# Two state recurrences written ahead of the score products in a step of gated linear attention

## The chip, the cores and the metric

The kernel runs on one core of a Trainium2 chip. The metric is the device time of one execution in microseconds (us); a kernel's time is the median of several executions. The engines of a core run side by side, each in the order of its own list of instructions, and wait for one another by semaphores: TensorE (PE; its weight loads are shown as PEld), VectorE (DVE), ScalarE (ACT), GpSimd (POOL) and SyncE (SP), which issues most of the DMAs.

## What is computed

Two layers of a streaming encoder over 1024 new frames and 64 frames of a running stream. In each layer half of the heads are gated linear attention (GLA), half are differential attention; a projection, a normalised residual and a convolutional feed-forward part follow. The change lies in GLA, which the reference computes in blocks of 64 tokens (cut):

```python
def gla_chunked(q, k, v, log_a, s0):
    G = jnp.cumsum(log_a, axis=-2)
    q_dec = q * jnp.exp(G)
    k_inv = k * jnp.exp(-G)
    k_end = k * jnp.exp(G_last - G)
    A = jnp.where(causal, jnp.einsum('nbhid,nbhjd->nbhij', q_dec, k_inv), 0.0)
    o_intra = jnp.einsum('nbhij,nbhjv->nbhiv', A, v)
    upd = jnp.einsum('nbhjd,nbhjv->nbhdv', k_end, v)
    decay = jnp.exp(G_last[..., 0, :])
    def step(S, inp):
        dec, u, qd = inp
        o = jnp.einsum('bhid,bhdv->bhiv', qd, S)
        return dec[..., None] * S + u, o
    s_final, o_inter = lax.scan(step, s0, (decay, upd, q_dec))
    o = o_intra + o_inter
```

The output is then normalised per head and multiplied by a gate. Everything is float32; the large projections are split into a high and a low part and computed in three passes of products.

## The kernel before

The kernel is one long program, with the order of every engine's work written out by hand. Python generators write it: a main loop writes blocks of large products, and between blocks a pump takes the next step of a generator that runs beside them, paced by an estimate of TensorE's and VectorE's time. The program's order on an engine is the order in which instructions are written. The waits between engines are put in from the order of writing: an instruction waits for what was written ahead of it in the program and touches the same memory. For PSUM a bank counts as a whole here, as the waits in the lists show.

`gla(l, p)` is such a generator. It runs four times, for layers 0 and 1 and for the pairs of heads p = 0 and 1, beside a projection's blocks of 24 products of 256 columns (`vd_block`, and at its end other projections). It has 15 steps, i = 0 to 14; a step writes some of ten stages, each for the tile of 128 tokens that lies `lag` steps back (nine tiles; the last is the running stream's). One step stands after each block of large products. The stages that matter here, with tile t:

- s0 (lag 0, TensorE): a transpose of the decayed keys, and two score products q·k of 128 columns, one for each head, into columns 0 to 127 of banks `bk(t, 0)` and `bk(t, 1)`. In the trace each float32 product is two passes, so s0's two products are four.
- s1 (lag 1, TensorE): the four products k·v that update the state, into columns 128 to 255 of the same two banks.
- v1 (lag 2, VectorE): two recurrences S = decay·S + update, the second from the result of the first, each reading columns 128 to 255 of one of the banks and writing a slot of the state (SR, a part of ACC).
- s2 (lag 2, TensorE): four products q·S from those states and two products of the masked scores with v, into columns 256 to 383.
- v2, v2b, v2c, s3 and v3 (lags 3 to 6): gating, the norm's power on GpSimd, scaling, transposes of the output, and their split into high and low parts.
- v0 (lag 0, VectorE and ScalarE): the masked copy of the scores out of both banks, and a copy of the transposed keys.

Banks alternate with the tile, so that the tiles i and i - 2 share theirs:

```python
        def bk(t, i):
            return 4 + 2 * (t % 2) + i
```

Beside the stages, VectorE also takes the low part of a weight (WL = RAW - WH, 128x1024) off its list where the pump puts it, behind v0 of two steps in each call.

Of the kernel before, what the change touches and what calls it, by code (L numbers as in the profile page):

```python
# [45 lines left out]
def hybrid_kernel(ctx: ExitStack, tc: tile.TileContext,  # L46
# [672 lines left out]
    def gla(l, p):  # L719
# [92 lines left out]
            V.scalar_tensor_tensor(ML[:, 2 * p:2 * p + 2, t0:t0 + n], src, gn, f(hi), ALU.mult, ALU.subtract)  # L812


        stages = ((s0, 0), (s1, 1), (v1, 2), (v2c, 5), (s2, 2), (v2b, 4), (s3, 6), (v2, 3), (v3, 6), (v0, 0))
        for i in range(9 + 6):
            for fn, lag in stages:
                if 0 <= i - lag < 9:
# [505 lines left out]
    for l in range(DEPTH):  # L1324
# [89 lines left out]
        def vd_block(s, t):  # L1414
            tm_block(L["vd%d" % s], t, 256, ev_vd(l, s, t))

        beside(gla(l, 0))
        for t in range(9):
            vd_block(0, t)
# [27 lines left out]
        drain()  # L1447
        ring["banks"] = (0, 1, 2)
        beside(gla(l, 1))
        pump()  # L1450
        for t in range(9):
# [175 lines left out]
```

## Time and profile before

| | us |
|---|---|
| median of 3 executions | 2831.58 (2826.98 to 2833.05) |
| the profiled execution | 2822.54 |
| its span, first to last instruction | 2820.8 |
| TensorE matmul busy, weight loads busy | 2779.2 (99%), 2709.6 (96%) |
| VectorE busy | 1695.0 (60%) |
| ScalarE busy | 1150.7 (41%) |
| chain that ended last: TensorE, VectorE | 92%, 2% |

In the profile an engine's busy time counts only its own operations, and the ends of matmuls are modelled. Idle time stands with the operation that follows it, with the engine that released it. The chain of work that ended last follows the program back from its last instruction, at each step to what released it.

### The profile page before, as it was taken

To read this page: it belongs to the slowest core of one execution; us is meant where nothing else is said; L and a number is where in the kernel's file an instruction comes from. 1 tells how busy PE (TensorE), PEld (TensorE's weight loads), DVE (VectorE), ACT (ScalarE), POOL (GpSimd) and SP (SyncE) were. 2 spreads that over 40 slices of the span, in tenths; PEclk is the share of its full clock that TensorE was granted. 3 is DMA by queue.
4 is the path that set the end of the run, shared out by engine and by line. 5 is a ranking of instruction groups with operands and counts; after the bars stand their busy time and mean duration, and the time that the engine had idled before them with its cause. 6 is when DMAs were issued, how large, how long until landed. Compare 5 with 4: busy or idle time off the path is not lost.

```text
span 2820.8 us, 46613 instructions
## 1 busy us (share of the span) xinstructions
PE 2779.2 (99%) x18407; PEld 2709.6 (96%) x18407; DVE 1695.0 (60%) x4104; ACT 1150.7 (41%) x2432; POOL 234.7 (8%) x387
## 2 busy tenths in 40 slices
PE   8999999999999999999999999999999999999999
PEld 8999888999999999999999898889999999999999
DVE  5443458477566666666772333685766666666665
ACT  5333348555322222222454242684552222222235
POOL 2200024200000000000021000340000000000000
PEclk9999999999999999999999999999999999999999
DMA  7421176341111111111352213834321111111122
GB/s 245 141 69 47 54 188 151 119 131 56 48 42 45 45 45 46 45 45 46 113 197 82 61 35 90 214 85 146 105 64 46 45 46 46 45 46 45 45 90 84
DMA packets 250690, 235.47 MB, mean 83 GB/s; under 512 B 12974, under 2 KB 225416, under 8 KB 250472
## 3 DMA queue, kind: packets, MB, share of 16 engines
q1 hardware_dynamic: 233032, 189.62, 23.4%
q0 software_dynamic: 10656, 39.07, 3.9%
q10 hardware_dynamic: 6784, 3.81, 0.5%
q8 instruction: 145, 2.38, 0.3%
q14 instruction: 73, 0.60, 0.1%
HBM read 174.34 MB, written 58.11 MB: 82 GB/s over the span
## 4 chain that ended last, share of the span: by engine, by line
PE 92%; DVE 2%; issue 2%; DMA 2%; ACT 1%; POOL 0%; SPq 0%; ACTq 0%; DVEq 0%; POOLq 0%
PE PS L103 89%; PE PS L107 3%; DVE ACC L122 1%; DVE SML L122 1%; DMA WH<-KSd 0%; ACT ACC L1070 0%; DMA XS<-ACC 0%; DMA RAW<-in_w_in_dram 0%; DMA WH<-QSd 0%; DMA out_dram<-TMP 0%; DVE TMP L122 0%; DMA QSd<-MH 0%; DVE ML L122 0%; ACT WH L275 0%; DMA ACC<-in_x_prompt_dram 0%
## 5 line engine op out<-in xcount | busy, mean ns | idle before, releaser
L103 PE MATMUL PS<-XL,WH 128*128 128x384 f32 (+1 forms) x2976 | 557.3, 326 | 0.0
L103 PEld LDWEIGHTS PS<-XL,WH 128*128 128x128 f32 x2976 | 499.2, 188 | 0.0
L103 PE MATMUL PS<-XH,WH 128*128 128x384 f32 (+1 forms) x2592 | 484.7, 328 | 3.4 <-DVE TMP L122 3.4
L103 PE MATMUL PS<-XH,WL 128*128 128x384 f32 (+1 forms) x2592 | 478.9, 326 | 0.0
L103 PEld LDWEIGHTS PS<-XH,WH 128*128 128x128 f32 x2592 | 433.8, 188 | 4.7 <-DVE TMP L122 4.3
L103 PEld LDWEIGHTS PS<-XH,WL 128*128 128x128 f32 x2592 | 433.7, 188 | 0.1
L103 PE MATMUL PS<-MH,WH 128*128 128x384 f32 (+1 forms) x1248 | 387.2, 329 | 0.0
L103 PE MATMUL PS<-MH,WL 128*128 128x384 f32 (+1 forms) x1248 | 385.1, 327 | 0.0
L103 PE MATMUL PS<-ML,WH 128*128 128x384 f32 (+1 forms) x1248 | 384.3, 327 | 0.0
L122 DVE TENSOR_TENSOR TMP<-PS,RB 128x384 f32<-128x384 f32 (+2 forms) x376 | 159.6, 444 | 343.2 <-PE PS L103 329.1
L275 ACT ACTIVATE WH<-RAW 128x1024 fp32r<-128x1024 f32 (+2 forms) x209 | 216.7, 1048 | 336.0 <-PE PS L103 300.1
L1237 ACT ACTIVATE TMP<-TMP,VC 128x384 f32<-128x384 f32 (+1 forms) x264 | 183.1, 694 | 404.3 <-DVE TMP L122 403.5
L122 DVE TENSOR_TENSOR ACC<-PS,ACC 128x384 f32<-128x384 f32 (+1 forms) x456 | 239.7, 533 | 133.4 <-PE PS L103 132.7
L122 DVE TENSOR_TENSOR WL<-RAW,WH 128x1024 fp32r<-128x1024 f32 (+2 forms) x209 | 253.9, 1216 | 98.6 <-ACT WH L275 98.6
L122 DVE SCALAR_TENSOR_TENSOR TMP<-TMP,VC 128x384 f32<-128x384 f32 (+1 forms) x528 | 311.8, 591 | 0.1
L103 PEld LDWEIGHTS PS<-MH,WL 128*128 128x128 f32 x1248 | 230.9, 188 | 0.0
L103 PEld LDWEIGHTS PS<-ML,WH 128*128 128x128 f32 x1248 | 230.9, 188 | 0.0
L103 PEld LDWEIGHTS PS<-MH,WH 128*128 128x128 f32 x1248 | 230.1, 188 | 0.7 <-issue 0.3
L122 DVE TENSOR_REDUCE SML<-PS 128x1 f32<-128x384 f32 (+6 forms) x144 | 104.3, 724 | 41.9 <-PE PS L103 40.4
L103 PE MATMUL PS<-WH,XH 128*128 128x256 f32 (+1 forms) x864 | 128.4, 291 | 0.0
L1258 ACT ACTIVATE MH<-TMP 128x384 fp32r<-128x384 f32 x132 | 67.0, 508 | 135.6 <-DVE TMP L122 135.5
L103 PE MATMUL PS<-WH,XL 128*128 128x256 f32 (+1 forms) x864 | 122.0, 284 | 0.0
(202 smaller groups left out, 3440.9 us busy)
## 6 DMA issues: line engine op xcount, KB each, us to landing
RAW<-in_w_ffn_up_dram SPq DMA_DIRECT2D x88, 512.0 KB
RAW<-in_w_in_dram SPq DMA_DIRECT2D x48, 512.0 KB
RAW<-in_w_ffn_down_dram SPq DMA_DIRECT2D x44, 512.0 KB
RAW<-in_w_out_dram SPq DMA_DIRECT2D x32, 512.0 KB
XH<-XS SPq DMA_DIRECT2D x8, 1536.0 KB
XS<-ACC POOLq DMA_DIRECT2D x6, 1536.0 KB, 6.8
XH<-KSd SPq DMA_DIRECT2D x32, 256.0 KB
XH<-XS SPq DMA_DIRECT2D x4, 1280.0 KB
```

Of the source, the lines that this page charges most:

```text
L103: nc.tensor.matmul(out, lhsT, rhs, **kw)
L107: nc.tensor.transpose(out, in_, idn)
L122: return op(out, *a, **kw)
L275: act(hi, src, AF.Copy)
L1237: act(c, e[:, 0:w], AF.Identity, bias=cb(l, u), scale=cw(l, 0, u))
L1258: act(MH[:, mid["j"] % 4, mid["t0"]:mid["t0"] + n], y[:, :n], AF.Copy)
```

## The change

In the list of stages v1 is written first in a step, ahead of s0 and s1, and no longer behind them:

```diff
@@ -812,7 +812,7 @@
-        stages = ((s0, 0), (s1, 1), (v1, 2), (v2c, 5), (s2, 2), (v2b, 4), (s3, 6), (v2, 3), (v3, 6), (v0, 0))
+        stages = ((v1, 2), (s0, 0), (s1, 1), (v2c, 5), (s2, 2), (v2b, 4), (s3, 6), (v2, 3), (v3, 6), (v0, 0))
         for i in range(9 + 6):
```

v1 is VectorE's (and a DMA's at the last two tiles), s0 and s1 are TensorE's, so no engine gets its instructions in another order: the lists of all five engines are the same, row for row, when waits are left out. With the waits shown, TensorE's and VectorE's lists differ, in the four calls of `gla`; those of ScalarE, GpSimd and SyncE do not.

On TensorE, step 2 of the first call (IDN is the identity of a transpose, ACC holds queries, keys, values and state, TMP the masked scores; 128x128 is a product of s0, the first four 64x128 are s1, the next four s2):

```order
 L107 MATMUL PS<-IDN,ACC 128x128 [waits Activation_49]
-L103 MATMUL PS<-ACC 128x128 x2
-L103 MATMUL PS<-ACC 64x128 [waits DVE_49]
-L103 MATMUL PS<-ACC 64x128 x3
-L103 MATMUL PS<-ACC 64x128 [waits DVE_49] x2
-L103 MATMUL PS<-ACC 64x128 x2
+L103 MATMUL PS<-ACC 128x128 [waits DVE_49] x2
+L103 MATMUL PS<-ACC 64x128 x8
 L103 MATMUL PS<-ACC,TMP 128x128 x2
 L103 MATMUL PS<-WH,XH 128x256 x8
```

The waits for VectorE have moved from s1 and s2 to the two products of s0.

On VectorE, v0 of step 3 and then step 4 of the first call (the masked copy is v0, the two operations on ACC, TMP and PS are v1, SML and OGT belong to v2b and v2):

```order
 L122 COPY_PREDICATED TMP<-MSK,PS 128x256 [waits PE_49]
-L122 SCALAR_TENSOR_TENSOR ACC<-ACC,TMP,PS 128x128 [waits PE_49]
-L122 SCALAR_TENSOR_TENSOR ACC<-ACC,TMP,PS 128x128 [waits DVE_49,PE_49]
+L122 SCALAR_TENSOR_TENSOR ACC<-ACC,TMP,PS 128x128 [waits DVE_49] x2
 L122 TENSOR_SCALAR SML<-SML 128x2
 L122 TENSOR_TENSOR OGT<-PS,ACC 128x256 [waits Activation_49]
```

Both recurrences lose their wait for TensorE.

On VectorE, behind v0 of step 6 and in step 7, where a weight split (WL) stands in between:

```order
 L122 COPY_PREDICATED TMP<-MSK,PS 128x256
 L122 TENSOR_TENSOR WL<-RAW,WH 128x1024 [waits DMAHW2_49]
-L122 SCALAR_TENSOR_TENSOR ACC<-ACC,TMP,PS 128x128 [waits DVE_49,PE_49] x2
+L122 SCALAR_TENSOR_TENSOR ACC<-ACC,TMP,PS 128x128 [waits DVE_49] x2
 L122 TENSOR_SCALAR OGT<-OGT,SML 128x128 [waits Pool_49]
```

The split keeps its place; again only the wait for TensorE is gone. In step 2 of a call, the first in which v1 has a tile, the recurrences keep a wait for TensorE.

## Rows read from the trace of the kernel before

**Rows 1.** The page: busy us, share, instructions; then the granted clock by slice.

```profile
PE 2779.2 (99%) x18407; PEld 2709.6 (96%) x18407; DVE 1695.0 (60%) x4104; ACT 1150.7 (41%) x2432; POOL 234.7 (8%) x387
...
PEclk9999999999999999999999999999999999999999
```

**Rows 2.** Busy time by stretch (first call; sum of four calls): stretch, length, engines, clock.

```profile
186.00:240.00 54.00, 53.45 (x490) 45.55 (x490) 20.56 (x61) 15.30 (x57) 4.88 (x7) 1.00 0.22 64
...
sum 214.00, PE 211.70 PEld 179.50 DVE 82.19 ACT 60.45 POOL 19.50; mean PE 52.92 PEld 44.87 DVE 20.55 ACT 15.11 POOL 4.87
```

**Rows 3.** The chain that ended last, step 3: start us, length us, what.

```profile
202.37 0.47 PE PS L103 x4
202.84 0.34 DVE ACC L122
...
203.23 0.43 PE PS L103 x2
```

**Rows 4.** Timeline, weight loads of TensorE: start, length, operation, count [idle before].

```profile
203.22 0.19 PEld L103 LDWEIGHTS PS<-ACC 64*64 64x64 f32 x2 [0.30 <-DVE ACC L122]
203.68 0.20 PEld L103 LDWEIGHTS PS<-ACC 64*64 64x64 f32 x6 [0.26 <-DVE ACC L122]
...
207.66 0.63 PEld L103 LDWEIGHTS PS<-ACC 64*128 64x128 f32 x12 [0.16 <-issue]
...
223.99 0.63 PEld L103 LDWEIGHTS PS<-ACC 64*128 64x128 f32 x12 [0.16 <-issue]
```

**Rows 5.** Waits of the weight loads, whole run, then first call: total us, times, longest.

```profile
PEld PS L103 <- DVE ACC L122: 16.2, 58, 0.3
...
PEld PS L103 <- DVE ACC L122: 3.9, 14, 0.3
```

**Rows 6.** Timeline of VectorE in the first call, steps 2 to 7.

```profile
199.78 1.21 DVE L122 TENSOR_TENSOR WL<-RAW,WH 128x1024 fp32r<-128x1024 f32 x1
202.82 0.80 DVE L122 SCALAR_TENSOR_TENSOR ACC<-ACC,TMP,PS 128x128 f32<-128x128 f32 x2 [1.84 <-PE PS L103]
...
204.80 0.45 DVE L122 COPY_PREDICATED TMP<-MSK,PS 128x256 f32<-128x256 uint8 x1 [0.32 <-PE PS L103]
...
222.36 1.21 DVE L122 TENSOR_TENSOR WL<-RAW,WH 128x1024 fp32r<-128x1024 f32 x1
224.52 0.80 DVE L122 SCALAR_TENSOR_TENSOR ACC<-ACC,TMP,PS 128x128 f32<-128x128 f32 x2 [0.94 <-PE PS L103]
```

**Rows 7.** Timeline of TensorE: starts of steps 0 to 4, and step 9 of the second call.

```profile
189.16 0.27 PE L107 MATMUL PS<-IDN,ACC 128*128 128x128 f32 x1
...
192.75 0.27 PE L107 MATMUL PS<-IDN,ACC 128*128 128x128 f32 x1
...
196.72 0.27 PE L107 MATMUL PS<-IDN,ACC 128*128 128x128 f32 x1
...
202.10 0.27 PE L107 MATMUL PS<-IDN,ACC 128*128 128x128 f32 x1
...
204.05 0.71 PE L103 MATMUL PS<-ACC,TMP 128*128 128x128 f32 x4
204.52 1.19 PE L103 MATMUL PS<-WH,XH 128*128 128x256 f32 x8
...
207.47 0.27 PE L107 MATMUL PS<-IDN,ACC 128*128 128x128 f32 x1
...
360.85 0.65 PE L103 MATMUL PS<-ACC 64*64 64x128 f32 x12
361.44 0.71 PE L103 MATMUL PS<-ACC,TMP 128*128 128x128 f32 x4
```

**Rows 8.** Start of attention, layer 0: chain, SyncE's timeline, SyncE's waits.

```profile
390.67 5.28 DMA WH<-KSd
...
390.18 1.08 SPq L1000 DMA_DIRECT2D WH<-KSd  x2
...
SPq L1000 <- PE PS L103: 11.8, 3, 7.1
```

## The prediction

> **What bounds the kernel now.** I read the page's first two parts, then the table of stretches, then the chain of work that ended last, and last the timelines of TensorE and VectorE inside one step. TensorE's weight loads fill 96% of the span and its clock is granted in full throughout [rows 1], so a microsecond is won only where TensorE stands still. The changed function runs four times, once per layer and pair of heads. In such a stretch VectorE is busy for 20.56 of 54 us [rows 2]: it is not the bound, and can only hurt by being asked too late.
>
> It is asked too late. In the chain [rows 3] a step reads: the score products s0 (four passes, 0.47 us), then 0.34 on VectorE, then two passes of s2 (0.43), and the rest on TensorE without a break. The piece on VectorE is the first state recurrence of v1. The second shows in the weight loads, which stop twice in a step, 0.30 and 0.26 us, each time until VectorE has written ACC [rows 4]. Over the whole run this wait is there 58 times and costs 16.2 us; a stretch has 14 of them [rows 5], two in each of seven steps. Four stretches hold 56; the other two stand before the first score products of the second calls and are not this step's. So there are 28 steps: the steps 2 to 8 of each call, in which s0 and v1 both have a tile.
>
> Why VectorE is late: the two recurrences begin at 202.82, after 1.84 us of idling that TensorE ended [rows 6], and s0 ends at 202.84 on the chain [rows 3]. v1 reads columns 128 to 255 of two PSUM banks, s0 writes columns 0 to 127 of the same two. The columns are disjoint, and v1's real inputs (s1 of the step before) are older by 24 large products. So v1 waits for the s0 that is written ahead of it, and s2, four products behind s0 on TensorE, waits for v1. After the change the order has it the other way: s0's two products wait for VectorE, and v1 no longer for TensorE.
>
> The Trainium skill, "PSUM — Partial Sum Buffer", section "PSUM bank collisions raise a hardware error", says to guard PSUM with semaphores by bank and quadrant, not by address. By that rule the wait can only turn round and never vanish, which speaks against the change; the trace agrees on the old direction, with the start at 202.82 beside the end at 202.84. By the rule alone the gain could be anything down to a loss, which is the second rival below.
>
> **The change part by part.** No instruction is added, removed or moved on any engine; only waits differ. SyncE, ScalarE and GpSimd keep rows and waits, so no DMA is moved past another.
>
> Removed: v1's wait for s0, and with it s2's wait for v1. What a step costs without it comes from TensorE's own rows [rows 7]. Step 0 (s0 alone) is 192.75 - 189.16 = 3.59 us long. Step 1 adds the eight passes of s1: 196.72 - 192.75 = 3.97, so these are 0.38. Step 3 adds s2, eight passes of the same kind, and four passes of the masked scores, 204.52 - 204.05 = 0.47. Unhindered that would be 3.97 + 0.38 + 0.47 = 4.82; it is 207.47 - 202.10 = 5.37. The difference is 0.55. Two readings agree: the two stops of the weight loads, 0.30 + 0.26 = 0.56 [rows 4], and step 9, where no s0 stands in the way and twelve passes of this kind, eight of them s2, take 361.44 - 360.85 = 0.59, so 0.39 for eight [rows 7]. I take 0.55: 28 x 0.55 = **15.4 us**. Steps 6 to 8, which also transpose outputs, have the same two stops and count in full.
>
> Added: s0's two products wait, each for the recurrence that reads its bank. That is free if v1 is done before TensorE arrives. v1 now follows the masked copy v0 of the step before directly. In an ordinary step that copy starts at 204.80 and lasts 0.45, the pair after it 0.80, so it is done by 206.05; s0's weights load at 207.66 [rows 4, 6]. The cover is **1.6 us**. In two steps of each call a weight split (WL) stands between the two: 199.78 + 1.21 + 0.80 = 201.79 on VectorE [rows 6], and s0 begins at 202.37 on the chain [rows 3], 0.6 to spare. In one of these two steps the output work of v3 stands ahead as well, and it is the tightest: split until 222.36 + 1.21 = 223.57, first recurrence done about 223.57 + 0.34 = 223.91, the second by 223.57 + 0.80 = 224.37; s0 loads at 223.99, and its second product follows by half of 0.47, near 224.23 [rows 3, 4, 6]. Only the second product waits, 0.1 to 0.2 us. One step per call is placed so: **0.4 to 0.8 us** in all, of which I take 0.5. If the cover were gone, each step would cost what the second rival says. These margins do not shrink when the stalls go: the copy v0 is itself released by TensorE's masked-score products, and the 24 large products between those and the next s0 keep their length.
>
> Queued behind v1 on VectorE are v2c, v2b and v2. The first two now run up to 3 us earlier, and what they wait for, GpSimd's power and ScalarE's sums, was asked for in the step before. v2 waits for ScalarE's squares as it did. TensorE's s1 and s2 need no wait of their own any more: their producers stand ahead of v1 on VectorE.
>
> Sum on the profiled execution: 2822.5 - 15.4 + 0.5 = 2807.6. That execution lies 9 us below the median of the three runs (2831.58, lowest 2826.98); the saving does not depend on that offset, so on the median it is 2831.6 - 14.9 = 2816.7, rounded to **2817 us**. At 4.82 us a step nothing of VectorE is late next; the next thing TensorE waits for is the start of attention.
>
> **The rivals.** First, **given back at the start of attention**. Behind the second call TensorE waits for keys, 5.28 us on the chain [rows 8]. If those transfers came at a time of their own, the 7.5 us saved in the two second calls would be waited away there and 7.5 would be left: 2824. Against it: SyncE issues that load at 390.18, 0.5 us before the wait begins on the chain, and what SyncE waits for at this line is TensorE, 11.8 us in three waits [rows 8]. So the transfers start earlier as TensorE does. Chance 0.09.
>
> Second, **slower: s0 is held by v1**. If VectorE came to the pair only when TensorE comes to s0, s0 would stand for 0.80 + 0.04, against 0.55 now at s2: 0.29 more in 28 steps, +8 us, 2840. It decides from the point where the pair ends over 0.55 us after s0 could start: if VectorE came to it 2.1 us later than in the rows of an ordinary step, 1.1 later with a split, 0.4 in the tightest. Its idling ahead of the pair, 1.84 us and still 0.94 in the tightest step, speaks against this [rows 6]. For it: a wait on TensorE that v1 kept would bring just that; step 2 keeps one, but for the s1 of the step before. Chance 0.05.
>
> Third, **nothing to win**. TensorE's row shows 211.70 busy of 214.00 us in the four stretches [rows 2]. Read literally, at most 2.3 us of idling can go: 2829. Against it: both stops of the weight loads lie inside time that this row calls busy [rows 2, 4]. Chance 0.06. The Trainium skill, "Trainium Kernel Development and Optimization", section "Performance Expectations", says that matmul busy time is a bad measure because matmuls are pipelined, and weight-load busy time a good one. By the one the gain would be under 2.3 us, by the other 56 stops of 0.28, some 15.7; the rows [rows 2, 4] agree with the page.
>
> **How the numbers follow.** Forecast 0.80, rivals 0.09, 0.05 and 0.06. Low end: all 16.2 us of [rows 5], and a median as low as the lowest run shown, 4.6 below: 2831.6 - 16.2 - 4.6 = 2810.8, put at 2810. High end: the give-back case, 2824, and a microsecond of scatter: 2825. About 0.2%, 5.7 us, is what a measurement of this kernel can tell from no change. Faster by more than that: the forecast and nearly all of the give-back case, 0.88. Within it: 0.07. Slower: 0.05.
>
> **What would show it.** Right: the weight loads' waits for ACC fall from 58 to a handful; a step of the pattern in [rows 7] is 4.8 us long; the pair starts right behind the copy or the split; each call is some 3.8 us shorter; the wait for keys stays near 5.3. Wrong: stops of 0.3 us or more at the score products (second rival), a wait for keys longer by 3 to 4 us (first), or steps still at 5.37 (third).

## The result, and the profile after

The changed kernel took 2809.55 us as the median of six runs (2804.08 to 2815.17), beside 2829.28 for the kernel before: a ratio of 0.993, 95% interval 0.9912 to 0.9949. In a second comparison it was 2812.42 against 2829.50, ratio 0.9937 (0.992 to 0.9953); one run of the kernel before that took 4853.79 us at a granted clock of 0.732 is left out of this median. It is faster, by 0.6 to 0.7%, 17.1 to 19.7 us. The forecast was faster by 14.9, with 2817 in a range from 2810 to 2825; the first median lies half a microsecond below that range, the second inside it.

The page of the profiled execution, whose span is 2808.5 us, which answers to [rows 1]:

```profile
PE 2766.1 (98%) x18407; PEld 2710.2 (96%) x18407; DVE 1690.2 (60%) x4104; ACT 1151.0 (41%) x2432; POOL 234.8 (8%) x387
```

What is left of the weight loads' waits for ACC (total us, times, longest), which answers to [rows 5]:

```profile
PEld PS L103 <- DVE ACC L122: 1.1, 6, 0.2
```

The stops went from 58 and 16.2 us to 6 and 1.1 us. TensorE in the first call, by start and length, which answers to [rows 7]; the rows are the starts of steps 0 to 3, then of 7 and 8 (the tight step is 7):

```profile
189.12 0.27 PE L107 MATMUL PS<-IDN,ACC 128*128 128x128 f32 x1
...
192.70 0.27 PE L107 MATMUL PS<-IDN,ACC 128*128 128x128 f32 x1
192.91 0.87 PE L103 MATMUL PS<-ACC 64*128 64x128 f32 x12
193.71 1.22 PE L103 MATMUL PS<-WH,XH 128*128 128x256 f32 x8
...
196.68 0.27 PE L107 MATMUL PS<-IDN,ACC 128*128 128x128 f32 x1
196.88 1.09 PE L103 MATMUL PS<-ACC 64*128 64x128 f32 x20
197.90 0.71 PE L103 MATMUL PS<-ACC,TMP 128*128 128x128 f32 x4
...
201.33 0.27 PE L107 MATMUL PS<-IDN,ACC 128*128 128x128 f32 x1
...
220.11 0.27 PE L107 MATMUL PS<-IDN,ACC 128*128 128x128 f32 x1
220.31 1.36 PE L103 MATMUL PS<-ACC 64*128 64x128 f32 x20
221.60 0.71 PE L103 MATMUL PS<-ACC,TMP 128*128 128x128 f32 x4
...
225.24 0.27 PE L107 MATMUL PS<-IDN,ACC 128*128 128x128 f32 x1
```

A full step is 201.33 - 196.68 = 4.65 us long, 4.64 in the next ones; before it was 5.37, and the forecast had 4.82. The 20 passes of s0, s1 and s2 take 197.90 - 196.88 = 1.02, the 12 of s0 and s1 in step 1 take 193.71 - 192.91 = 0.80: s2's eight are 0.22. In the tight step 7 the 20 take 221.60 - 220.31 = 1.29, 0.27 more.

VectorE in the same call, steps 2 to 3 and 6 to 7, which answers to [rows 6]:

```profile
198.65 0.45 DVE L122 COPY_PREDICATED TMP<-MSK,PS 128x256 f32<-128x256 uint8 x1 [4.03 <-PE PS L103]
198.99 1.21 DVE L122 TENSOR_TENSOR WL<-RAW,WH 128x1024 fp32r<-128x1024 f32 x1
200.12 0.72 DVE L122 SCALAR_TENSOR_TENSOR ACC<-ACC,TMP,PS 128x128 f32<-128x128 f32 x2
...
218.68 1.21 DVE L122 TENSOR_TENSOR WL<-RAW,WH 128x1024 fp32r<-128x1024 f32 x1
219.81 0.72 DVE L122 SCALAR_TENSOR_TENSOR ACC<-ACC,TMP,PS 128x128 f32<-128x128 f32 x2
```

The pair no longer idles for TensorE: it runs right behind the split, in 0.72 instead of 0.80. In step 3 it is done at 200.84, 0.7 us before s0; in step 7 only at 220.53, with s0 due at 220.31. What that costs is read from single weight loads (the timeline in narrow windows): s0's four and the first of s1 in step 2, then s0's four and the last two of them in step 7.

```profile
196.88 0.30 PEld L103 LDWEIGHTS PS<-ACC 64*128 64x128 f32 x4 [0.16 <-issue]
197.30 0.13 PEld L103 LDWEIGHTS PS<-ACC 64*64 64x64 f32 x1
...
220.31 0.57 PEld L103 LDWEIGHTS PS<-ACC 64*128 64x128 f32 x4 [0.16 <-DVE ACC L122]
220.59 0.29 PEld L103 LDWEIGHTS PS<-ACC 64*128 64x128 f32 x2
```

In step 2 the two products of s0 run side by side, four loads in 0.30 us. In step 7 the second product starts at 220.59, behind the second recurrence, and each runs alone: 0.57, the 0.27 that the step is longer. In step 2 the loads also stand for 0.12 us between s0's last, which ends at 197.18, and the first of s1, where their shape changes.

Where the whole time went is read by cutting the span at the first and the last 64-row product of each call. The four calls together, from the starts of those records: 204.43 us before (50.18, 52.02, 50.20, 52.03) and 185.09 after (45.35, 47.19, 45.35, 47.20). **That is 19.3 us, 4.8 in each call.** Between first and second call of a layer there are 75.08 us in both kernels. The two spans differ by only 12.3, since the pieces behind the second calls, which hold the start of attention, came out longer in this pair: 1212.4 and 1058.3 us before, 1216.6 and 1061.1 after. Whether that belongs to the change is the second question below.

### The profile page after: what moved, and what is told of

It is laid out like the page before. It is cut to its first block, busy times and chain, and to the rows that moved or that the text cites. A ratio compares the mean times of both kernels' runs of the same rounds, so it can differ in the third digit from the quotient of the medians.

```text
span 2808.5 us, 46577 instructions
## 1 busy us (share of the span) xinstructions
PE 2766.1 (98%) x18407; PEld 2710.2 (96%) x18407; DVE 1690.2 (60%) x4104; ACT 1151.0 (41%) x2432; POOL 234.8 (8%) x387
## 4 chain that ended last, share of the span: by engine, by line
PE 92%; DMA 2%; DVE 2%; issue 2%; ACT 1%; POOL 0%; SPq 0%; ACTq 0%; DVEq 0%; POOLq 0%
PE PS L103 89%; PE PS L107 3%; DVE SML L122 1%; DMA out_dram<-TMP 1%; DVE ACC L122 1%; DMA WH<-QSd 0%; ACT ACC L1070 0%; DMA WH<-KSd 0%; DMA VSd<-TMP 0%; DMA QSd<-MH 0%; DVE TMP L122 0%; ACT WH L275 0%; DVE ML L122 0%; SPq L992 0%; DMA ACC<-in_x_prompt_dram 0%
```

## The experiments

Two things were open: why a step saved 0.73 us and not 0.55, and whether the start of attention gives part of the saving back. The table gives each kernel's ratio to the kernel before; the columns from the third on are worked out from TensorE's records in its profiled execution.

| kernel | ratio to before (95%) | four calls, us | call 2 to call 3, us | call 4 to the last product, us |
|---|---|---|---|---|
| before | | 204.43 | 1212.4 | 1058.3 |
| again_before | 1.0003 (0.9993 to 1.0014) | 204.41 | 1216.5 | 1063.4 |
| kout2_before | 0.9982 (0.9972 to 0.9992) | 204.48 | 1214.1 | 1058.1 |
| after | 0.993 (0.9912 to 0.9949) | 185.09 | 1216.6 | 1061.1 |
| again_after | 0.9937 (0.992 to 0.9953) | 185.14 | 1221.2 | 1066.0 |
| s1_alt | 0.993 (0.9913 to 0.9947) | 185.18 | 1216.5 | 1060.5 |
| kout2 | 0.9923 (0.991 to 0.9937) | 185.17 | 1213.0 | 1059.0 |
| s0_quad | 0.9921 (0.9906 to 0.9936) | 178.47 | 1218.7 | 1060.2 |
| v1_end | 0.9949 (0.9933 to 0.9964) | 184.01 | 1216.9 | 1061.3 |
| v1_end2 | 0.992 (0.9899 to 0.994) | 184.06 | 1219.1 | 1062.0 |
| best | 0.9934 (0.9921 to 0.9946) | 177.35 | 1221.5 | 1065.3 |
| best2 | 0.9903 (0.9883 to 0.9924) | 177.36 | 1218.2 | 1058.6 |

**Both kernels once more.** No edit.

> The kernel before, once more, against itself. It serves two ends. Its ratio shows what a comparison of this kind can tell: 1.000, with an interval of about 0.2% to either side. And its profile is a second look at the place where the first pair of profiles lost time again: if the loss of 5.4 us at the start of attention in layer 0 (between the end of the second call and the keys' arrival) belongs to the change, this profile has it as small as the first of before, with the wait of ScalarE for the store of the keys' output near 3.5 us; if it is scatter of that store's landing, the wait may be anything from 2 to 8 us here too.

> The changed kernel, once more. The steps say: 28 steps, each shorter by 5.37 - 4.64 = 0.73 us, less 0.27 in the four tight ones, so 19.3 us, ratio 0.9932. If the start of attention gives a part back in every run (theory of the give-back), the ratio is nearer to 0.9956, the 12.3 us by which the two profiles' spans differ; if the give-back is scatter, it is 0.993 and this profile's span may be 5 us or more beside the first.

The calls repeat to 0.1 us; the pieces with attention do not, in either kernel. Waits of ScalarE for the store of the keys' output (line 902), and of TensorE's transposes for what comes behind it; first the two profiles of the changed kernel, then the second of the kernel before:

```profile
ACT TMP L902 <- DMA out_dram<-TMP: 12.9, 2, 7.6
PE PS L107 <- DVE TMP L122: 6.3, 2, 4.1
```

```profile
ACT TMP L902 <- DMA out_dram<-TMP: 15.4, 2, 7.8
PE PS L107 <- DVE TMP L122: 8.5, 2, 4.3
```

```profile
ACT TMP L902 <- DMA out_dram<-TMP: 10.2, 2, 6.6
PE PS L107 <- DVE TMP L122: 3.5, 2, 3.1
```

In the first profile of before these waits were 7.5 and 0.5 us, and in s1_alt below, whose calls are as short as the changed kernel's, 7.4 and 1.0. So a loss of this kind is there in the kernel before too, and its size changes from one execution to the next. The 0.9956 of the give-back theory lies outside both intervals of the changed kernel.

**s0 in 64x64 loads.** On the changed kernel:

```diff
-            for h in range(2):
-                hp = slice(64 * h, 64 * h + 64)
-                mm(PS[:, bk(t, h), 0:128], E[1][hp, tok], E[0][hp, tok], start=True, stop=True)
+            for c in range(2):
+                cp = slice(64 * c, 64 * c + 64)
+                ct = slice(tt(t) + 64 * c, tt(t) + 64 * c + 64)
+                for h in range(2):
+                    hp = slice(64 * h, 64 * h + 64)
+                    mm(PS[cp, bk(t, h), 0:128], E[1][hp, ct], E[0][hp, tok], start=True, stop=True)
```

> The changed kernel, with each score product of 128 output rows written as two of 64, so that s0 uses 64x64 weight loads as s1 and s2 do. The prediction's term for s2 was too large: it took s1's eight passes as 0.38 us and s2's as the same, and they took 0.22. Two theories. (a) Change of shape: the array stands still for about 0.16 us when the shape of the loads changes, s1 pays that once behind s0 and s2, of s1's shape, does not. Then s0 with 64x64 loads takes the change away from between s0 and s1: a full step falls from 4.64 to about 4.48 us, 28 to 32 steps, 4.5 to 6 us in all against the changed kernel, about 25 us or 0.9912 against the kernel before. (b) Halves: s2 is cheap because its products alternate between the two halves of the array's rows and overlap. Then s0 gains nothing, since its two products are on different halves already, and has twice the passes: step 4.64 or longer, ratio 0.993 or above.

TensorE's timeline of this kernel, steps 0, 1 and 2:

```profile
188.81 0.27 PE L107 MATMUL PS<-IDN,ACC 128*128 128x128 f32 x1
189.01 0.45 PE L103 MATMUL PS<-ACC 64*64 64x128 f32 x8
189.39 1.22 PE L103 MATMUL PS<-WH,XH 128*128 128x256 f32 x8
...
192.37 0.27 PE L107 MATMUL PS<-IDN,ACC 128*128 128x128 f32 x1
192.57 0.67 PE L103 MATMUL PS<-ACC 64*64 64x128 f32 x16
193.16 1.21 PE L103 MATMUL PS<-WH,XH 128*128 128x256 f32 x8
...
196.13 0.27 PE L107 MATMUL PS<-IDN,ACC 128*128 128x128 f32 x1
196.33 0.89 PE L103 MATMUL PS<-ACC 64*64 64x128 f32 x24
197.15 0.71 PE L103 MATMUL PS<-ACC,TMP 128*128 128x128 f32 x4
...
200.58 0.27 PE L107 MATMUL PS<-IDN,ACC 128*128 128x128 f32 x1
```

Eight passes of one shape take 0.38, sixteen 0.59, twenty-four 0.82: 0.21 to 0.23 for each eight beyond the first, and some 0.16 that does not depend on their number. The full step is 200.58 - 196.13 = 4.45, although s0 has twice the passes. The four calls lost another 6.6 us. The new form of s0 is not cheaper by itself: step 0, where s0 stands alone, is 192.37 - 188.81 = 3.56 us long, beside 192.70 - 189.12 = 3.58 in the changed kernel. So the change of shape between s0 and s1 had cost about 0.2 us a step, as theory (a) says; theory (b) forecast no gain.

**s1 in the other order.** The four products with h as the outer loop:

```diff
-            for c in ((0, 1) if t < 8 else (1,)):
-                rp = slice(64 * c, 64 * c + 64)
-                for h in range(2):
-                    hp = slice(64 * h, 64 * h + 64)
+            for h in range(2):
+                hp = slice(64 * h, 64 * h + 64)
+                for c in ((0, 1) if t < 8 else (1,)):
+                    rp = slice(64 * c, 64 * c + 64)
```

> The changed kernel, with s1's four products in the other order, so that neighbours lie on different halves of the array's rows, as s2's do. (a) Change of shape: nothing changes, the step stays at 4.64 us and the ratio at that of the changed kernel (0.993). (b) Halves: s1's eight passes fall from 0.38 to 0.22, a step from 4.64 to 4.48, 32 steps, 5 us in all, ratio about 0.9914.

```profile
197.14 0.27 PE L107 MATMUL PS<-IDN,ACC 128*128 128x128 f32 x1
197.34 1.09 PE L103 MATMUL PS<-ACC 64*128 64x128 f32 x20
198.36 0.71 PE L103 MATMUL PS<-ACC,TMP 128*128 128x128 f32 x4
...
201.79 0.27 PE L107 MATMUL PS<-IDN,ACC 128*128 128x128 f32 x1
```

The step is 4.65 and the 20 passes 1.02, as without the edit. The halves theory falls.

**A second staging tile for the keys' output**, on the changed kernel and on the kernel before:

```diff
-                    act(KOUT, PS[:, b2, 0:384], AF.Copy)
+                    ko = SQ[:, 0:384] if (h, g) == (3, 1) else KOUT
+                    act(ko, PS[:, b2, 0:384], AF.Copy)
...
-                                      KOUT.rearrange("p (a c) -> p a c", a=3))
+                                      ko.rearrange("p (a c) -> p a c", a=3))
```

> The changed kernel, with the keys' output of head 3, middle group, staged in a free tile (SQ) instead of the one staging tile that the store of the first group still holds. In the four profiles so far ScalarE waits 7.4 to 15.4 us in all for that store at the two starts of attention, and behind it VectorE and TensorE. Theory of the give-back: the calls shortened by the change bring TensorE to the start of attention earlier than the stores allow, so that a part of the 19.4 us is lost there; then taking this wait away gives the changed kernel 4 to 8 us more (2804 or less, ratio 0.990 to 0.9915), and clearly more than it gives the kernel before. Theory of scatter: the store lands early or late whatever the kernel; the gain is 1 to 4 us and the same for both kernels, ratio 0.992 to 0.993. In either case the waits for the store at that line go to zero and TensorE's waits for VectorE's TMP at its transposes fall under 1 us.

> The kernel before, with the same second staging tile. Theory of the give-back: little, 0 to 2 us (ratio 0.9993 to 1.000), since this kernel comes to the start of attention late enough. Theory of scatter: the same 1 to 4 us as for the changed kernel (0.9985 to 0.9996).

The kernel before gained 4.9 us by the medians (2825.20 against 2830.08), the changed kernel about 2 to 5 (2807.73, beside 2809.55 and 2812.42 in the earlier comparisons, with overlapping intervals). What ended ScalarE's idling ahead of this line in the changed kernel with the second tile:

```profile
L903 ACT ACTIVATE SQ<-PS x2: 490/490/490, 371.2 to 1751.9; 128x384 f32<-128x384 f32 x2
its engine sat idle before it (us, times) until:
  PE PS L107: 10.4, 6
```

No wait for the store is left. The give-back theory wanted 4 to 8 us for the changed kernel and 0 to 2 for the one before; the second half failed plainly. So nothing here shows that this wait is a price of the change: it costs either kernel a few microseconds, more in one execution than in another. With the second tile in both kernels the pieces behind the second calls are alike in the two profiles (1213.0 and 1059.0 us changed, 1214.1 and 1058.1 before), and the medians are 17.5 us apart. Part of that scatter also showed in the intervals: the runs of kout2_before reach from 2823.88 to 2829.19, those of again_before from 2826.33 to 2835.5.

**v1 at the end of a step.** Behind v0, for the tile one step back, so ahead of the weight split on VectorE:

```diff
-        stages = ((v1, 2), (s0, 0), (s1, 1), (v2c, 5), (s2, 2), (v2b, 4), (s3, 6), (v2, 3), (v3, 6), (v0, 0))
+        stages = ((s0, 0), (s1, 1), (v2c, 5), (s2, 2), (v2b, 4), (s3, 6), (v2, 3), (v3, 6), (v0, 0), (v1, 1))
```

> The changed kernel with v1 written at the end of a step, behind v0, for the tile one step back: the same place on VectorE but ahead of the weight split instead of behind it. The four tight steps took 4.91 us where 4.64 stands without a split, 0.27 more (the prediction had 0.1 to 0.2). If that is s0's wait for the second recurrence, the four come down to the length of their neighbours and the kernel gains 1.1 us, 0.9928 against 0.9932, which only the profile can show. Rival: it is the split itself (the weights read by TensorE, or memory shared with VectorE); then the tight steps keep their 0.27.

Each call became 0.24 to 0.29 us shorter, so the 0.27 of the tight step was s0's wait. Yet by the median, 2815.84, the kernel was slower than the changed one, with overlapping intervals (0.9933 to 0.9964 beside 0.9912 to 0.9949). v1 also carries DMAs, the stores of the state at the last two tiles, and they had moved with it. SyncE's timeline of v1_end, and then a wait of TensorE's transposes that the changed kernel has only 0.3 us of:

```profile
351.18 0.33 SPq L753 DMA_DIRECT2D out_dram<-ACC  x1
351.60 0.38 SPq L989 DMA_DIRECT2D WL<-BND  x1
```

```profile
PE PS L107 <- DVE ML L122: 4.6, 2, 2.4
```

The store of line 753 (the running stream's state, the last tile) now stands ahead of attention's loads, which begin at 351.60, 2.5 us before the call's last 64-row product at 354.1. In the changed kernel they began at 351.57, 5.4 us before that product at 356.9. The chain of v1_end runs on from this store over the load of the queries (5.73 us from 353.95) and a store of values (3.41 from 359.70) to VectorE's ML and the transposes, which begin at 365.88 after 2.27 us of waiting. To test this, the last two tiles kept their place:

```diff
+        def v1a(t):
+            if t < 7:
+                v1(t)
+        def v1b(t):
+            if t >= 7:
+                v1(t)
-        stages = ((s0, 0), (s1, 1), (v2c, 5), (s2, 2), (v2b, 4), (s3, 6), (v2, 3), (v3, 6), (v0, 0), (v1, 1))
+        stages = ((v1b, 2), (s0, 0), (s1, 1), (v2c, 5), (s2, 2), (v2b, 4), (s3, 6), (v2, 3), (v3, 6), (v0, 0), (v1a, 1))
```

> As v1_end, but the recurrences of the last two tiles, which carry the two stores of the state, stay where the changed kernel has them, so that SyncE's queue keeps its order. In v1_end the calls got 0.27 us shorter each, as expected, and yet the kernel came out at 0.9949, some 5 us slower than the changed kernel. Theory of the queue: the store of the prompt's state, which v1_end puts ahead of the loads for attention on SyncE, holds those up (they were issued 2.6 us before the end of the second call, 5.4 in the changed kernel), so with the stores back in place the loss goes and 0.9925 to 0.9935 is left. Theory of the early arrival: whatever shortens the second call is lost at the start of attention; then it stays at 0.994 to 0.996 here too.

SyncE's timeline of v1_end2, and TensorE's row of the step that was tight:

```profile
349.60 0.40 SPq L997 DMA_DIRECT2D WL<-BND  x1
...
358.95 0.53 SPq L753 DMA_DIRECT2D out_dram<-ACC  x1
```

```profile
218.87 1.09 PE L103 MATMUL PS<-ACC 64*128 64x128 f32 x20
```

The store is behind the loads again, the tight step has the length of its neighbours, and the ratio is 0.992 against 0.9949. The two intervals overlap a little (0.9933 to 0.9964 and 0.9899 to 0.994), and the two profiled executions do not show the gain: the pieces behind the second calls are longer in v1_end2 (1219.1 and 1062.0 us beside 1216.9 and 1061.3), which had 7.3 us of waits behind the store of the keys' output where v1_end had 0.7. So by this pair alone the queue is likely and not proved; the pair of combinations below, whose second staging tile takes those waits away, points the same way.

**The parts together**: s0 in 64x64 loads, the second staging tile, and v1 at the end of a step, with the stores moved (best) and in place (best2).

> Changed kernel with 64x64 score products, v1 at the end of a step and the second staging tile together. If the parts add up: 19.4 from the calls, 32 x 0.20 = 6.4 from the shape of s0's loads, 1.1 from the tight steps, and 1 to 6 from the staging tile: 28 to 33 us, 2797 to 2802, ratio 0.9884 to 0.9901. If the start of attention swallows what comes before it, 0.992 or more.

> Changed kernel with 64x64 score products, the recurrences of the first seven tiles at the end of a step, stores in place, and the second staging tile. Theory of the queue: the parts add up to 19.3 + 6.5 + 1.1 and 2 to 5 from the staging tile, 29 to 32 us, 2798 to 2801, ratio 0.9887 to 0.9898. Theory of the early arrival: about 0.992 to 0.9935, as the first combination (0.9934).

best came out at 2811.07 us, best2 at 2801.20, with calls of the same length to 0.01 us. TensorE's transposes waited 5.7 us for VectorE's ML in best, where best2 has 0.5, and the pieces behind the second calls are 10.1 us shorter in best2 (1218.2 and 1058.6 beside 1221.5 and 1065.3). The intervals still overlap by a hair (0.9921 to 0.9946 and 0.9883 to 0.9924). best2 is at 0.9903, 28 us off the kernel before and, by the medians, some 8 to 11 off the changed kernel. The parts would have added up to 29 to 32.

## Where the prediction was right, and where it failed

- **What bounded the kernel, and the mechanism**: right. v1 had waited for the s0 written ahead of it, and s2 for v1. With v1 first, VectorE's pair begins behind the copy or the split, and the weight loads' stops for ACC are gone but for the six of 1.1 us: two at the first score products of the second calls, as before, and one of 0.16 in each tight step, the length that every step has there. The order of writing alone did it; no engine's list changed.
- **The size of a step's saving**: wrong, and this is the term that put the result outside the range. It was taken as 0.55 and is 0.73, 5.37 - 4.64. The step of the working that failed is "s2, eight passes of the same kind" at 0.38, read from what s1 had added in step 1. That 0.38 held one stop, for the change from 64x128 to 64x64 loads; s2 follows s1 in the same shape and pays none: its eight passes are 0.22 in the changed kernel, and in s0_quad eight more passes cost 0.21 to 0.23. 28 x (0.38 - 0.22) = 4.5 us is nearly the whole difference between 15.4 and the 20.4 that 28 steps of 0.73 make. The low end of the range went wrong with it: it took the 16.2 us of the stops as the most that could go, and the calls lost 19.3.
- **The two readings that agreed were not independent proof.** The stops of the weight loads, 0.30 + 0.26, counted only the idling. The passes beside them were slower too: the loads took 0.63 + 0.19 + 0.20 = 1.02 busy in three pieces before ([rows 4] shows the last two for step 3) and 0.85 in one piece after, and 0.56 + 0.17 = 0.73. Step 9's 0.59 was spread evenly over twelve passes; in s0_quad sixteen of one shape took that long, so a pass was priced too high there as well.
- **The tight steps**: place and count right, four in all, size too small: 0.27 each, 1.1 us, against 0.4 to 0.8. The reading that failed is that the second product follows the first by half of 0.47: in an ordinary step the two start together, so the second waited from 220.31 to 220.59, and the two no longer ran side by side. 28 x 0.73 - 4 x 0.27 = 19.4, and the calls lost 19.3.
- **Margins elsewhere**: right. In step 3, with a split ahead, the pair was done 0.7 us before s0, where 0.6 had been read off.
- **Given back at the start of attention**: a wait there did grow in the first pair of profiles, but not the one named. The keys' wait that stood for it did not grow (4.01 us on the chain, where it was 5.28); it was ScalarE's wait for the store of the keys' output. Timeline of the changed kernel:

```profile
377.68 0.49 ACT L902 ACTIVATE TMP<-PS 128x384 f32<-128x384 f32 x1 [7.62 <-DMA out_dram<-TMP]
...
380.14 0.90 PE L107 MATMUL PS<-IDN,TMP 128*128 128x128 f32 x3 [4.15 <-DVE TMP L122]
```

  In the first profile of before the same line had waited 3.51 us. Without the change the wait reached 6.6 us too (again_before), and kout2_before gained 4.9 us by taking it away. What of the 19.3 us is lost there on average is not settled: the medians say 17.1 to 19.7.
- **s0 held by v1, nothing to win**: neither came. TensorE's row was as misleading as the rival's own paragraph said: it counted 211.70 of 214.00 us busy, and 19.3 us went.

The Trainium skill, "TensorEngine Tiling (Array Packing)", section "When to Use Tiling", has row tiling in two for a contraction of 64 and column tiling in two for 64 output rows. s0 contracts over 64 and gives 128 output rows, so by that section it is a case for row tiling alone. s0_quad neither bears out nor contradicts this: step 0, where s0 stands alone, gained 0.02 us, and a full step 0.20. The price of changing from one shape to another, 0.16 to 0.2 us, is from the runs.

## What to carry to other kernels

Where waits follow the order of writing and a PSUM bank counts as one, two operations on different columns of a bank wait for each other, and the one written first goes first. Write first the one whose inputs are old and whose result is wanted soon, and read the cover on its engine's timeline; if the stage issues DMAs, leave those where they were. When a group of small matmuls is priced from another group, take the price from neighbours of the same load shape, or the change of shape is counted twice.

## What was not expected of the hardware

- Changing the shape of TensorE's loads between small groups costs some 0.16 to 0.2 us here, as much as six or seven further passes of 64x64 by 128 columns (0.22 for eight). Twice the passes in one shape were 0.20 us a step faster.
- A wait that stops TensorE twice costs more than the two gaps that the weight loads show: 0.56 of idling was 0.73 of time, since passes that ran side by side were broken up.
- The store of 128x384 float32 issued at 367.74 held its staging tile until 377.6, 9.9 us. The same store was free after about 5.8 us in the first profile of before, with the DMA engines as busy (0.96 and 278 GB/s in 375 to 385), and after 6.3 in s1_alt, where it was issued at 367.80. What makes it late is open. Behind it TensorE stood for 4.15 us, and the clock granted in that stretch fell to 0.70, part of it at the lower of the two levels (1.2 of 2.4 GHz), so that eight products that take 1.43 us before took 2.50. The kernel before had such a fall a little later, to 0.67 in 395 to 405, behind its wait for the keys. The changed kernel's two stretches:

```profile
365.00:375.00 10.00, 9.97 (x62) 9.50 (x61) 4.69 (x15) 2.50 (x7) 4.37 (x6) 1.00 0.92 251
375.00:385.00 10.00, 5.85 (x24) 5.03 (x23) 2.88 (x6) 2.81 (x7) 2.73 (x4) 0.70 0.43 139
```

  The columns are the stretch, its length, busy us of TensorE's products and loads, VectorE, ScalarE and GpSimd, then the granted clock, the DMA engines' busy share and GB/s.
